# A fused QKV projection on one NeuronCore: block-product columns 504 wide in rows of 512, direct columns 288 wide in two banks

## The chip, the cores and the metric

The kernel runs on one core of one Trainium2 chip. The metric is the device time of one execution in microseconds (us). Three runs of the kernel before the change took 362.86, 363.02 and 363.09 us; their median, 363.02 us, is the time that the change is measured against.

## The reference

```python
"x": np.random.randn(16, 512, 768).astype(np.float32)
"w_qkv": np.random.randn(768, 3 * 768).astype(np.float32)

def reference(x, w_qkv):
    qkv = np.matmul(x, w_qkv)
    hidden = x.shape[-1]
    q = qkv[..., :hidden]
    k = qkv[..., hidden:2*hidden]
    v = qkv[..., 2*hidden:]
    return np.stack([q, k, v], axis=0).astype(np.float32)
```

So 8192 rows of 768 elements are multiplied by a weight of 768 by 2304, and the 2304 result columns are stored as three outputs of 768 columns each.

## The kernel before

**Rows.** The 8192 rows are worked off in 32 pairs of 128 rows (`NP` = 32, index `p`). The contraction of 768 is cut into six slices of 128 (`KT` = 6), or two halves of three (`KH` = 3).

**Columns.** The 2304 columns are cut into five ranges: two groups (`q` = 0 and 1) of two column blocks each, a block being `CB` = 512 columns, and between the groups a remainder of `REM` = 2304 - 4 * 512 = 256 columns, the *direct columns*. Group 0 starts at column 0, the direct columns at 1024, group 1 at 1280.

**First stage.** The first three row pairs (`NS` = 3) are multiplied plainly, in bf16, by `block` (line 375): for each of the four column blocks there are six row tiles of six matmuls (line 385). While it runs, the weights arrive and are turned into what the main stage needs: bf16 copies `b1`, a copy `b22` and four sums and differences `t` of weight blocks (`sum_w`, line 105), the last two kinds in float32r, a 4-byte type.

**Main stage.** The other 29 row pairs (p = 3 to 31) use a scheme with seven block products instead of eight: the pair's 256 rows and a group's 1024 columns are a two by two arrangement of blocks (a `Quad`), and `do(u, n)` (line 220) makes product `n` by `product` (line 201), three matmuls into one PSUM bank each (line 212). Products 1 and 2 take bf16 operands (`xb`, `b1`), products 3 to 7 float32r operands (sums of x blocks in `s`, and `t` or `b22`). A pass over one row pair handles both groups (`two`, line 275; `last`, line 309, for the final pair), so it has 2 x 7 x 3 = 42 block-product matmuls, of which 30 are float32r and 12 bf16. ScalarE copies results out of PSUM (lines 226, 233, 239, 243), VectorE adds others on top (lines 230, 240, 246), into an output tile `o` of 2 x 1024 columns, which `store_quad` (line 251) stores by two DMAs on SyncE's queue.

**Direct columns.** In every pass `rem(p)` (line 267) makes the 256 direct columns in bf16 without the scheme: `rem_row` (line 260) issues six matmuls for each of the two row tiles, 12 in all (line 262). Both row tiles lie in one PSUM bank of 512 float32 (`[P, 2, REM]`), and one ScalarE instruction copies them out (line 272).

**Order.** The order on each engine is that of the program text (a manual schedule). PSUM banks come from one pool of eight, `ps_pool`, in rotation: a pass takes seven (two for `x`, one for the direct columns, two for `z`, two for `y`). A bank is given out again when the last reader of its former content is done. In a pass the order on TensorE is: products 1 of both groups, the direct columns, products 2, 6, then 5, 7, 5, 7, then 4, 3 of group 0 and 4, 3 of group 1.

**Start.** Before the first data are there, TensorE multiplies a tile of zeros (`busy`, line 361: 11 matmuls, later 4 more), between the transposes of the first two row pairs (`turn_rows`, line 160).

**SBUF layout.** The tiles `b1`, `b22`, `t` and the pool `tq` start at multiples of 2048 bytes of a partition; the bf16 weights of the direct columns lie in two tiles, `w_rem0` before `b1` and `w_rem1` in a pool of its own ahead of the pool of `s`.

Of the kernel before, what the change touches and what calls it, by code (L numbers as in the profile page):

```python
# [10 lines left out]
def kernel(  # L11
# [20 lines left out]
    nc = tc.nc  # L32
    P = 128
# [5 lines left out]
    KT = K // P  # L39
    KH = KT // 2  # L40
    KC = K // 4
    NP = M // (2 * P)
    CB = 512
    REM = N3 - 4 * CB
    Q_OFF = (0, 2 * CB + REM)
    R_OFF = 2 * CB
    fp32 = mybir.dt.float32
    f32r = mybir.dt.float32r
    bf16 = mybir.dt.bfloat16
    ident = mybir.ActivationFunctionType.Identity  # L50
    add = mybir.AluOpType.add
# [13 lines left out]
    xin_pool = ctx.enter_context(tc.tile_pool(name="xin", bufs=3))  # L65
    xf_pool = ctx.enter_context(tc.tile_pool(name="xf", bufs=2))
    xb_pool = ctx.enter_context(tc.tile_pool(name="xb", bufs=4))
    rem_pool = ctx.enter_context(tc.tile_pool(name="rem", bufs=1))
    s_pool = ctx.enter_context(tc.tile_pool(name="s", bufs=2))
    ps_pool = ctx.enter_context(tc.tile_pool(name="ps", bufs=8, space=bass.MemoryType.PSUM))  # L70

# [1 line left out]

    tiny = w_pool.tile([P, 1], fp32, name="tiny")
    eye = w_pool.tile([P, 176], bf16, name="eye")[:, :P]
    w_rem = [w_pool.tile([P, KH, REM], bf16, name="w_rem0"), None]

    b1 = [w_pool.tile([P, KT, CB], bf16, name=f"b1_{q}") for q in range(2)]
    b22 = [w_pool.tile([P, KH, CB], f32r, name=f"b22_{q}") for q in range(2)]
    t_0 = w_pool.tile([P, 4, KH, CB], f32r, name="t_0")  # L80
    w_rem[1] = rem_pool.tile([P, KH, REM], bf16, name="w_rem1")
    ts = [[t_0[:, n] for n in range(4)], None]


# [2 lines left out]
    def load_w(dst, j0, nj, off, cols):  # L87
        rows = w_qkv.rearrange("(p j) n -> p j n", j=KT)
        nc.sync.dma_start(dst, rows[:, j0:j0 + nj, off:off + cols])

    stage = {}

    def load_blocks(q, c, nj=KH):
        if q == 0:
            t = tq_pool.tile([P, KT, CB], fp32, name="st0", tag="tq")
            for j in range(0, KT, nj):
                load_w(t[:, j:j + nj], j, nj, Q_OFF[q] + c * CB, CB)
            stage[q, 0, c], stage[q, 1, c] = t[:, :KH, :], t[:, KH:, :]
        else:
            for h in range(2):  # L100
                t = st_pool.tile([P, KH, CB], fp32, name="st1", tag="st")
                load_w(t[:], h * KH, KH, Q_OFF[q] + c * CB, CB)
                stage[q, h, c] = t[:]

    def sum_w(q, n):
        t1, t2, t3, t4 = ts[q]
# [8 lines left out]
    xin, xf, xb, sr = {}, {}, {}, {}  # L115
# [78 lines left out]
    def quad(p, q):  # L194
        u = Quad()
        u.p, u.q = p, q
        u.o = o_pool.tile([P, 2, 2 * CB], fp32, name="o", tag="o")
        u.x = u.y = u.z = None
        return u

    def product(u, n, ps, start):
        t1, t2, t3, t4 = ts[u.q]
        if n <= 2:
            h = (n - 1) * KH
            lhs = [xb[u.p][:, h + j, :P] for j in range(KH)]
            rhs = [b1[u.q][:, h + j, :] for j in range(KH)]
        else:
            k, t = {3: (4, b22[u.q][:]), 4: (0, t4), 5: (1, t1), 6: (2, t2), 7: (3, t3)}[n]
            lhs = [sr[u.p][:, k, j, :] for j in range(KH)]
            rhs = [t[:, j, :] for j in range(KH)]  # L210
        for j in range(KH):
            nc.tensor.matmul(  # L212
                ps[:], lhs[j], rhs[j],
                start=(start and j == 0), stop=(j == KH - 1), skip_group_check=True,
            )

    def bank():
        return ps_pool.tile([P, CB], fp32, name="ps")

    def do(u, n):  # L220
        c11, c12 = u.o[:, 0, :CB], u.o[:, 0, CB:]
        c21, c22 = u.o[:, 1, :CB], u.o[:, 1, CB:]
        if n == 1:
            u.x = bank()
            product(u, 1, u.x, True)
            nc.scalar.activation(c11, u.x[:], ident)  # L226
        elif n == 2:
            u.z = bank()
            product(u, 2, u.z, True)
            nc.vector.tensor_tensor(c11, c11, u.z[:], op=add)  # L230
        elif n == 6:
            product(u, 6, u.x, False)
            nc.scalar.activation(c12, u.x[:], ident)  # L233
        elif n == 5:
            u.y = bank()
            product(u, 5, u.y, True)
        elif n == 7:
            product(u, 7, u.x, False)
            nc.scalar.activation(c22, u.x[:], ident)  # L239
            nc.vector.tensor_tensor(c22, c22, u.y[:], op=add)  # L240
        elif n == 4:
            product(u, 4, u.x, False)
            nc.scalar.activation(c21, u.x[:], ident)  # L243
        elif n == 3:
            product(u, 3, u.y, False)
            nc.vector.tensor_tensor(c12, c12, u.y[:], op=add)  # L246
# [13 lines left out]
    def rem_row(p, r, ps):  # L260
        for j in range(KT):
            nc.tensor.matmul(  # L262
                ps, xb[p][:, j, r * P:(r + 1) * P], w_rem[j // KH][:, j % KH, :],
                start=(j == 0), stop=(j == KT - 1), skip_group_check=True,
            )

    def rem(p):
        ps = ps_pool.tile([P, 2, REM], fp32, name="ps")
        for r in range(2):
            rem_row(p, r, ps[:, r, :])  # L270
        o = or_pool.tile([P, 2, REM], fp32, name="orem")
        nc.scalar.activation(o[:], ps[:], ident)  # L272
        nc.sync.dma_start(rows_of(1, p, R_OFF - H, R_OFF - H + REM), o[:])

    def two(a, b, early):
# [33 lines left out]
    def last(a, b):  # L309

        p = a.p

        def rem_stored(r):
            ps = bank()
            rem_row(p, r, ps[:, :REM])
            o = or_pool.tile([P, 2, REM], fp32, name="orem")
            nc.scalar.activation(o[:, 0, :], ps[:, :REM], ident)  # L317
# [24 lines left out]


    NS = 3
    zero = xb_pool.tile([P, CB], bf16, name="zero", tag="xb")
    nc.vector.memset(zero[:], 0.0)  # L346
    load_rows(0)
    nc.scalar.activation(tiny[:], zero[:, :1], ident)
# [26 lines left out]
    def block(q, c, w, groups, cast_next):  # L375


        ps = {}
        for js, tiles in groups:
            for n in tiles:  # L380
                p, r = divmod(n, 2)
                if n not in ps:
                    ps[n] = bank()
                for j in js:
                    nc.tensor.matmul(  # L385
                        ps[n][:], xb[p][:, j, r * P:(r + 1) * P], w[:, j, :],
                        start=(j == 0), stop=(j == KT - 1), skip_group_check=True,
                    )
# [5 lines left out]
                nc.scalar.activation(u.o[:, r, c * CB:(c + 1) * CB], ps[n][:], ident)  # L394
                if c == 1 and r == 1:
                    store_quad(u)

# [28 lines left out]
    act.activation(w_rem[1][:], st_rem[:, KH:], ident)  # L426
    dve.tensor_copy(out=w_rem[0][:], in_=st_rem[:, :KH])
    bt0 = bt_pool.tile([P, KT, CB], bf16, name="bt")
    bt1 = bt_pool.tile([P, KT, CB], bf16, name="bt")

    block(0, 0, b1[0], singles, nothing)
    rem(0)
# [5 lines left out]
        cast(0, h, 1, bt0, dve)  # L438
    for n in range(1, 5):
        sum_w(0, n)  # L440
    dve.tensor_copy(out=b22[0][:], in_=stage[0, 1, 1])
# [5 lines left out]
    t_1 = [tq_pool.tile([P, 2, KH, CB], f32r, name=f"t_1{n}", tag="tq") for n in range(2)]  # L447
    ts[1] = [t_1[n // 2][:, n % 2] for n in range(4)]
    sum_w(1, 1)
    sum_w(1, 2)  # L450
# [2 lines left out]
    sums_x(3)  # L453
    sum_w(1, 3)
    sum_w(1, 4)
    dve.tensor_copy(out=b22[1][:], in_=stage[1, 1, 1])

    for p in range(NS, NP):
        def early():
# [41 lines left out]
```

## Time and profile before

| | |
|---|---|
| median of 3 runs | 363.02 us |
| span of the profiled execution, first to last instruction | 361.3 us |
| between the two | 1.7 us |
| TensorE busy | 353.4 us (98%) |
| VectorE, ScalarE, GpSimd busy | 224.4, 182.9, 173.9 us (62, 51, 48%) |
| float32r block-product matmuls, 128x512 (line 212) | 870 in the program |
| bf16 matmuls, 128x512 (lines 212 and 385) | 348 and 144 in the program |
| bf16 matmuls of the direct columns, 128x256 (line 262) | 384 in the program |
| granted TensorE clock | 1.000 over the span |

One profiled execution gives all rows but the first and the counts. Matmuls are pipelined: the duration of a matmul's record is longer than the time until the next one starts, so costs of matmuls are read below as the step from one start to the next. A few matmul records are missing from the trace (28 of 348 bf16 records of line 212), so a group of 42 may show 41. In the timeline and chain views the first column is the start in us from the span's start, the second the length in us, and xN the number of instructions merged into the line.

### The profile page before, as it was taken

The page shows a single profiled execution, that of the slowest core. Times are in us where ns is not written, and L with a number is a line of the kernel's source. Part 1 is how long each engine was busy: PE and PEld are TensorE (multiplying, and loading weights), DVE is VectorE, ACT ScalarE, POOL GpSimd, SP SyncE. Part 2 cuts the span into 40 slices and gives each one's busy share as a digit, 9 for nine tenths or more (in the row PEclk, how much of TensorE's full clock was granted, in tenths as well). Part 3 has the DMA queues.
Part 4 walks back from the last instruction along what each step waited for, and adds up shares of the span by engine and source line. Part 5 has one row for each costly group of instructions (what it writes and reads, how often), then busy time and mean ns, then how long its engine had stood idle before and what let it go on. Part 6 is the DMA issues. An engine that isn't in the chain of part 4 may idle for free.

```text
span 361.3 us, 5221 instructions
## 1 busy us (share of the span) xinstructions
PE 353.4 (98%) x1765; PEld 251.0 (69%) x1797; DVE 224.4 (62%) x239; ACT 182.9 (51%) x304; POOL 173.9 (48%) x180
## 2 busy tenths in 40 slices
PE   8999999999999999999999999999999999999995
PEld 3644577777777777777777777777777777777763
DVE  3499826765566765566675565676556676556642
ACT  4547555455454545454545445455545454545452
POOL 0001861746664445664445665444665444666410
PEclk9999999999999999999999999999999999999999
DMA  7999869988898999899899999998989899999666
GB/s 298 405 388 373 286 221 359 331 289 295 278 328 301 294 273 294 276 324 315 280 280 290 281 308 309 291 289 278 292 288 321 295 300 271 297 272 339 264 261 232
DMA packets 80617, 108.08 MB, mean 299 GB/s; under 512 B 4816, under 2 KB 60368, under 8 KB 80592
## 3 DMA queue, kind: packets, MB, share of 16 engines
q1 hardware_dynamic: 65184, 96.35, 80.8%
q10 hardware_dynamic: 15408, 11.41, 9.6%
q8 instruction: 14, 0.23, 0.3%
q14 instruction: 11, 0.09, 0.1%
HBM read 32.24 MB, written 75.50 MB: 298 GB/s over the span
## 4 chain that ended last, share of the span: by engine, by line
PE 96%; ACT 1%; issue 1%; ACTq 0%; DVE 0%
PE ps L212 75%; PE ps L262 11%; PE ps L385 9%; PE ps L365 1%; PE ps L167 1%; ACT o L243 0%; ACTq L303 0%; ACT xb L147 0%; ACT orem L317 0%; DVE xb L145 0%; ACT xc L147 0%; ACTq L319 0%; DVE zero L346 0%; ACTq L317 0%
## 5 line engine op out<-in xcount | busy, mean ns | idle before, releaser
L212 PE MATMUL ps<-t,s 128*128 128x512 f32 x696 | 173.8, 398 | 0.0
L212 PEld LDWEIGHTS ps<-t,s 128*128 128x128 f32 x696 | 130.7, 188 | 29.7
L175 POOL CAST xb<-xf 128x1536 bf16<-128x1536 f32 x29 | 43.8, 1510 | 168.3 <-DVE xf L130 156.0
L240 DVE TENSOR_TENSOR o<-o,ps 128x512 f32<-128x512 f32 x58 | 39.9, 688 | 91.2 <-ACT o L239 91.2
L130 DVE STREAM_TRANSPOSE xf<-xin 128x1536 f32<-128x1536 f32 x29 | 85.5, 2950 | 3.7 <-DMA out_dram<-orem 2.1
L212 PE MATMUL ps<-b,xb 128*128 128x512 bf16 x320 | 82.4, 380 | 1.5
L239 ACT ACTIVATE o<-ps 128x512 f32<-128x512 f32 x58 | 34.8, 600 | 44.2 <-PE ps L212 44.2
L212 PEld LDWEIGHTS <-xb 128*128 128x128 bf16 x348 | 31.7, 98 | 35.6 <-issue 7.3
L233 ACT ACTIVATE o<-ps 128x512 f32<-128x512 f32 x58 | 34.9, 601 | 42.1 <-PE ps L212 39.4
L246 DVE TENSOR_TENSOR o<-o,ps 128x512 f32<-128x512 f32 x58 | 39.9, 688 | 21.3 <-PE ps L212 20.2
L212 PE MATMUL ps<-b,s 128*128 128x512 f32 x174 | 48.7, 389 | 0.0
L262 PE MATMUL ps<-w_rem,xb 128*128 128x256 bf16 x384 | 47.2, 273 | 0.0
L243 ACT ACTIVATE o<-ps 128x512 f32<-128x512 f32 x58 | 34.7, 599 | 24.1 <-PE ps L212 21.3
L226 ACT ACTIVATE o<-ps 128x512 f32<-128x512 f32 x58 | 34.7, 598 | 23.8 <-DVE o L246 20.6
L262 PEld LDWEIGHTS <-xb 128*128 128x128 bf16 x384 | 37.4, 98 | 11.2 <-issue 0.5
L230 DVE TENSOR_TENSOR o<-o,ps 128x512 f32<-128x512 f32 x58 | 36.5, 673 | 5.4 <-PE ps L212 4.1
L212 PEld LDWEIGHTS ps<-b,s 128*128 128x128 f32 x174 | 32.7, 188 | 6.8
L184 POOL TENSOR_TENSOR s<-s,xf 128x384 fp32r<-128x384 f32 x29 | 30.0, 1035 | 2.3
L183 POOL TENSOR_TENSOR s<-xf 128x384 fp32r<-128x384 f32 x29 | 30.9, 1064 | 0.0
L185 POOL TENSOR_TENSOR s<-xf 128x384 fp32r<-128x384 f32 x29 | 29.5, 1017 | 0.0
L187 POOL TENSOR_TENSOR s<-xf,s 128x384 fp32r<-128x384 f32 x29 | 29.5, 1016 | 0.0
L272 ACT ACTIVATE orem<-ps 128x512 f32<-128x512 f32 x31 | 18.5, 598 | 20.7 <-PE ps L262 19.5
(36 smaller groups left out, 129.4 us busy)
## 6 DMA issues: line engine op xcount, KB each, us to landing
out_dram<-o SPq DMA_DIRECT2D x62, 768.0 KB, 4.8
out_dram<-o SPq DMA_DIRECT2D x65, 256.0 KB, 4.1
xin<-in_x_dram SPq DMA_DIRECT2D x62, 192.0 KB, 6.9
xin<-in_x_dram ACTq DMA_DIRECT2D x54, 192.0 KB, 4.4
out_dram<-orem SPq DMA_DIRECT2D x31, 256.0 KB, 5.7
st<-in_w_qkv_dram SPq DMA_DIRECT2D x6, 768.0 KB, 13.1
xin<-in_x_dram SPq DMA_DIRECT2D x3, 768.0 KB, 5.7
st<-in_w_qkv_dram SPq DMA_DIRECT2D x6, 256.0 KB, 6.1
```

The source lines that it names most:

```text
L130: nc.vector.transpose(t[:].rearrange("p j (g b) -> p g j b", b=G), xin.pop(p)[:].rearrange("p g (a j) -> p g j a", a=G),)
L175: nc.gpsimd.tensor_copy(out=xb[p][:], in_=xf[p][:])
L212: nc.tensor.matmul(ps[:], lhs[j], rhs[j], start=(start and j == 0), stop=(j == KH - 1), skip_group_check=True,)
L226: nc.scalar.activation(c11, u.x[:], ident)
L230: nc.vector.tensor_tensor(c11, c11, u.z[:], op=add)
L233: nc.scalar.activation(c12, u.x[:], ident)
L239: nc.scalar.activation(c22, u.x[:], ident)
L240: nc.vector.tensor_tensor(c22, c22, u.y[:], op=add)
L243: nc.scalar.activation(c21, u.x[:], ident)
L246: nc.vector.tensor_tensor(c12, c12, u.y[:], op=add)
L262: nc.tensor.matmul(ps, xb[p][:, j, r * P:(r + 1) * P], w_rem[j // KH][:, j % KH, :], start=(j == 0), stop=(j == KT - 1), skip_group_check= ...
L385: nc.tensor.matmul(ps[n][:], xb[p][:, j, r * P:(r + 1) * P], w[:, j, :], start=(j == 0), stop=(j == KT - 1), skip_group_check=True,)
```

## The change

`CB`, the width of a column block, becomes 504, and a new `CP` = 512 is the pitch: every tile that holds column blocks keeps rows of 512 elements, of which 504 are used. `REM` becomes 2304 - 4 * 504 = 288. Two row tiles of 288 columns need 576 float32 and no longer fit one bank, so `rem` takes one bank for each row tile and ScalarE copies each out by itself; a pass now takes eight banks. The two `w_rem` tiles become one, which is filled up so that the tiles behind it still start at multiples of 2048 bytes; the pool `rem` goes. The second batch of start-up matmuls (4 bf16 of 512 columns) becomes 4 float32r matmuls of 496, 496, 480 and 480 columns on a new tile of zeros, which GpSimd fills first of all. The outputs' stores have the same number of DMAs; pieces that were 256 columns wide are 240, 264 or 288.

```diff
-    CB = 512
+    CB = 504
+    CP = 512
     REM = N3 - 4 * CB
...
-    rem_pool = ctx.enter_context(tc.tile_pool(name="rem", bufs=1))
...
-    w_rem = [w_pool.tile([P, KH, REM], bf16, name="w_rem0"), None]
-
-    b1 = [w_pool.tile([P, KT, CB], bf16, name=f"b1_{q}") for q in range(2)]
-    b22 = [w_pool.tile([P, KH, CB], f32r, name=f"b22_{q}") for q in range(2)]
-    t_0 = w_pool.tile([P, 4, KH, CB], f32r, name="t_0")
-    w_rem[1] = rem_pool.tile([P, KH, REM], bf16, name="w_rem1")
+    w_rem = w_pool.tile([P, 7 * P * 2], bf16, name="w_rem")[:, :KT * REM]
+    w_rem = w_rem.rearrange("p (h j c) -> p h j c", h=2, j=KH)
+    w_rem = [w_rem[:, h] for h in range(2)]
+
+    b1 = [w_pool.tile([P, KT, CP], bf16, name=f"b1_{q}")[:, :, :CB] for q in range(2)]
+    b22 = [w_pool.tile([P, KH, CP], f32r, name=f"b22_{q}")[:, :, :CB] for q in range(2)]
+    t_0 = w_pool.tile([P, 4, KH, CP], f32r, name="t_0")[:, :, :, :CB]
...
-        u.o = o_pool.tile([P, 2, 2 * CB], fp32, name="o", tag="o")
+        u.o = o_pool.tile([P, 2, 2 * CP], fp32, name="o", tag="o")[:, :, :2 * CB]
...
-    def bank():
-        return ps_pool.tile([P, CB], fp32, name="ps")
+    def bank(n=CB):
+        return ps_pool.tile([P, CP], fp32, name="ps")[:, :n]
...
     def rem(p):
-        ps = ps_pool.tile([P, 2, REM], fp32, name="ps")
+        o = or_pool.tile([P, 2, REM], fp32, name="orem")
         for r in range(2):
-            rem_row(p, r, ps[:, r, :])
-        o = or_pool.tile([P, 2, REM], fp32, name="orem")
-        nc.scalar.activation(o[:], ps[:], ident)
+            ps = bank(REM)
+            rem_row(p, r, ps)
+            nc.scalar.activation(o[:, r, :], ps, ident)
         nc.sync.dma_start(rows_of(1, p, R_OFF - H, R_OFF - H + REM), o[:])
...
-    zero = xb_pool.tile([P, CB], bf16, name="zero", tag="xb")
+    zeros = bt_pool.tile([P, 2 * CP], f32r, name="zeros", tag="bt")
+    nc.gpsimd.memset(zeros[:].bitcast(mybir.dt.uint32), 0)
+    zero = xb_pool.tile([P, CP], bf16, name="zero", tag="xb")
...
-            nc.tensor.matmul(ps[:], zero[:, :P], zero[:], start=True, stop=True)
+            nc.tensor.matmul(ps, zero[:, :P], zero[:, :CB], start=True, stop=True)
+
+    def busy_rounded():
+
+        ps = bank()
+        for n in (496, 496, 480, 480):
+            nc.tensor.matmul(
+                ps[:, :n], zeros[:, CP:CP + P], zeros[:, :n], start=True, stop=True
+            )
...
-    busy(4)
+    busy_rounded()
```

More of the change, by code (lines that the diff above doesn't have):

```diff
@@ L94, in load_blocks @@
         if q == 0:
-            t = tq_pool.tile([P, KT, CB], fp32, name="st0", tag="tq")
+            t = tq_pool.tile([P, KT, CP], fp32, name="st0", tag="tq")[:, :, :CB]
             for j in range(0, KT, nj):
@@ L100, in load_blocks @@
             for h in range(2):
-                t = st_pool.tile([P, KH, CB], fp32, name="st1", tag="st")
-                load_w(t[:], h * KH, KH, Q_OFF[q] + c * CB, CB)
-                stage[q, h, c] = t[:]
+                t = st_pool.tile([P, KH, CP], fp32, name="st1", tag="st")[:, :, :CB]
+                load_w(t, h * KH, KH, Q_OFF[q] + c * CB, CB)
+                stage[q, h, c] = t
     def sum_w(q, n):
@@ L207, in product @@
         else:
-            k, t = {3: (4, b22[u.q][:]), 4: (0, t4), 5: (1, t1), 6: (2, t2), 7: (3, t3)}[n]
+            k, t = {3: (4, b22[u.q]), 4: (0, t4), 5: (1, t1), 6: (2, t2), 7: (3, t3)}[n]
             lhs = [sr[u.p][:, k, j, :] for j in range(KH)]
@@ L212, in product @@
             nc.tensor.matmul(
-                ps[:], lhs[j], rhs[j],
+                ps, lhs[j], rhs[j],
                 start=(start and j == 0), stop=(j == KH - 1), skip_group_check=True,
             )
-    def bank():
-        return ps_pool.tile([P, CB], fp32, name="ps")
+    def bank(n=CB):
+        return ps_pool.tile([P, CP], fp32, name="ps")[:, :n]
     def do(u, n):
@@ L225, in do @@
             product(u, 1, u.x, True)
-            nc.scalar.activation(c11, u.x[:], ident)
+            nc.scalar.activation(c11, u.x, ident)
         elif n == 2:
@@ L229, in do @@
             product(u, 2, u.z, True)
-            nc.vector.tensor_tensor(c11, c11, u.z[:], op=add)
+            nc.vector.tensor_tensor(c11, c11, u.z, op=add)
         elif n == 6:
             product(u, 6, u.x, False)
-            nc.scalar.activation(c12, u.x[:], ident)
+            nc.scalar.activation(c12, u.x, ident)
         elif n == 5:
@@ L238, in do @@
             product(u, 7, u.x, False)
-            nc.scalar.activation(c22, u.x[:], ident)
-            nc.vector.tensor_tensor(c22, c22, u.y[:], op=add)
+            nc.scalar.activation(c22, u.x, ident)
+            nc.vector.tensor_tensor(c22, c22, u.y, op=add)
         elif n == 4:
             product(u, 4, u.x, False)
-            nc.scalar.activation(c21, u.x[:], ident)
+            nc.scalar.activation(c21, u.x, ident)
         elif n == 3:
             product(u, 3, u.y, False)
-            nc.vector.tensor_tensor(c12, c12, u.y[:], op=add)
+            nc.vector.tensor_tensor(c12, c12, u.y, op=add)
     def rows_of(s, p, lo, hi):
@@ L313, in rem_stored @@
         def rem_stored(r):
-            ps = bank()
-            rem_row(p, r, ps[:, :REM])
+            ps = bank(REM)
+            rem_row(p, r, ps)
             o = or_pool.tile([P, 2, REM], fp32, name="orem")
-            nc.scalar.activation(o[:, 0, :], ps[:, :REM], ident)
+            nc.scalar.activation(o[:, 0, :], ps, ident)
             row = (2 * p + r) * P
@@ L385, in block @@
                     nc.tensor.matmul(
-                        ps[n][:], xb[p][:, j, r * P:(r + 1) * P], w[:, j, :],
+                        ps[n], xb[p][:, j, r * P:(r + 1) * P], w[:, j, :],
                         start=(j == 0), stop=(j == KT - 1), skip_group_check=True,
@@ L393, in block @@
                 u = quads[q][p]
-                nc.scalar.activation(u.o[:, r, c * CB:(c + 1) * CB], ps[n][:], ident)
+                nc.scalar.activation(u.o[:, r, c * CB:(c + 1) * CB], ps[n], ident)
                 if c == 1 and r == 1:
@@ L425 @@
         cast_k(j)
[L426 to L429, printed above, removed]
+    act.activation(w_rem[1], st_rem[:, KH:], ident)
+    dve.tensor_copy(out=w_rem[0], in_=st_rem[:, :KH])
+    bt0 = bt_pool.tile([P, KT, CP], bf16, name="bt")[:, :, :CB]
+    bt1 = bt_pool.tile([P, KT, CP], bf16, name="bt")[:, :, :CB]
     block(0, 0, b1[0], singles, nothing)
@@ L440 @@
         sum_w(0, n)
-    dve.tensor_copy(out=b22[0][:], in_=stage[0, 1, 1])
+    dve.tensor_copy(out=b22[0], in_=stage[0, 1, 1])
     block(0, 1, bt0, halves(range(6)), cast_next(1, 0, b1[1]))
@@ L446 @@
     rem(2)
-    t_1 = [tq_pool.tile([P, 2, KH, CB], f32r, name=f"t_1{n}", tag="tq") for n in range(2)]
+    t_1 = [
+        tq_pool.tile([P, 2, KH, CP], f32r, name=f"t_1{n}", tag="tq")[:, :, :, :CB] for n in range(2)
+    ]
     ts[1] = [t_1[n // 2][:, n % 2] for n in range(4)]
@@ L455 @@
     sum_w(1, 4)
-    dve.tensor_copy(out=b22[1][:], in_=stage[1, 1, 1])
+    dve.tensor_copy(out=b22[1], in_=stage[1, 1, 1])
     for p in range(NS, NP):
```

## The prediction

> **What bounds the kernel now.** I read the page's busy shares first, then the chain of work that ended last, then that chain in order of time, and last the timeline of TensorE and its weight loads inside one pass.
>
> ```profile
> PE 353.4 (98%) x1765; PEld 251.0 (69%) x1797; DVE 224.4 (62%) x239; ACT 182.9 (51%) x304; POOL 173.9 (48%) x180
> PE 96%; ACT 1%; issue 1%; ACTq 0%; DVE 0%
> PEclk9999999999999999999999999999999999999999
> ```
>
> TensorE is busy for 98% of the span, and 96% of the chain is its own work, at the full granted clock throughout. No other engine is above 62%. What the change is worth is therefore the sum of TensorE's own steps, unless something else comes to hold TensorE up.
>
> ```profile
> 9.46 2.16 PE ps L385 x10
> 57.47 1.31 PE ps L262 x12
> 58.83 9.38 PE ps L212 x41
> 68.21 1.31 PE ps L262 x12
> 69.57 9.38 PE ps L212 x41
> ```
>
> This is the chain in order of time. Ten bf16 matmuls of 512 columns take 2.16 us: 216 ns from one start to the next. Twelve bf16 matmuls of 256 columns take 1.31 us: 109.2 ns each. A pass is 68.21 - 57.47 = 10.74 us, and 69.57 + 9.38 = 78.95 is the next pass's start, so passes follow each other without a hole. In a pass 12 x 109.2 ns are direct columns (1.31 us) and 12 x 216 ns are products 1 and 2 (2.59 us); the other 30, in float32r, share 10.74 - 1.31 - 2.59 = 6.84 us, or 228.0 ns each. Between the same width in bf16 and in float32r there are thus 12 ns, and the two timelines below show that these are not a constant.
>
> ```profile
> 64.70 0.84 PE L212 MATMUL ps<-b,s 128*128 128x512 f32 x3
> 65.38 0.84 PE L212 MATMUL ps<-t,s 128*128 128x512 f32 x3
> 66.06 0.84 PE L212 MATMUL ps<-b,s 128*128 128x512 f32 x3
> 66.74 1.47 PE L212 MATMUL ps<-b,xb 128*128 128x512 bf16 x6
> 68.05 1.47 PE L262 MATMUL ps<-w_rem,xb 128*128 128x256 bf16 x12
> ```
>
> ```profile
> 59.91 1.57 PEld L212 LDWEIGHTS ps<-t,s 128*128 128x128 f32 x7
> 61.75 2.68 PEld L212 LDWEIGHTS ps<-t,s 128*128 128x128 f32 x12
> ```
>
> Late in a pass three float32r matmuls take 0.68 us (64.70, 65.38, 66.06): 226.7 ns each. The weight loads, which start with the matmul before them and last 0.19 us, tell the same: the twelve from 61.75 on are (2.68 - 0.19) / 11 = 226 ns apart, but the first seven of the pass (1.57 - 0.19) / 6 = 230 ns. Equal instructions of equal shape first wander around 230 ns and then settle at 226.7 ns. The records' durations (shortest, median, longest) show the same, from 60.1 us on and from 62.2 us on:
>
> ```profile
> L212 PE MATMUL ps<-t,s x7: 387/393/397, 60.1 to 61.5; 128*128 128x512 f32 x7
> L212 PE MATMUL ps<-t,s x14: 389/389/389, 62.2 to 65.8; 128*128 128x512 f32 x14
> ```
>
> **The change part by part: what the widths do.** One column in bf16 costs (216 - 109.2) / 256 = 0.417 ns, so 8 columns are 3.3 ns and 32 columns 13.3 ns. Counts are the program's, over all passes and the first stage.
>
> Direct columns: 384 matmuls go from 256 to 288 columns, 109.2 to 122.5 ns: 384 x 13.33 ns = +5.12 us. All of them stand on the chain, none is hidden.
>
> bf16 blocks: 348 in products 1 and 2 and 144 in the first stage lose 8 columns: 492 x 3.33 ns = -1.64 us.
>
> float32r products: 870 matmuls lose 8 columns. This decides, since the two terms above leave +3.48 us, and 3.48 us / 870 = 4.0 ns is what each of them has to save for the kernel to stay even. No row shows a float32r matmul of any width but 512, so I bound it. From above: the step doesn't follow the width and stays where it was (226.7 settled, 228.0 on average), saving nothing; it can even lose, if it never settles and stays at the 230 ns of the pass's first seven (+2.0 ns). From below: the whole excess over bf16 goes and the step is 216 - 3.3 = 212.6 ns, a saving of 15.4 ns. In between, the plain reading from the nearest row, in proportion or with a fixed excess, saves 3.3 to 3.5 ns. I do not take the plain reading, because the excess is neither: it varies between instructions of one shape and then locks. The settled 226.7 ns is 34 times 6.67 ns, the time of 16 columns at 0.417 ns; all widths of the kernel so far are multiples of 16 columns, and 8 columns are half of that. If the step settles on such multiples, the next places are 33 (220.0 ns) and 34 (226.7 ns). I take 220.0, also nearly the middle of 212.6 and 226.7: -6.67 ns x 870 = -5.80 us. This is a choice between ends far apart, and the range keeps both.
>
> The sum is 5.12 - 1.64 - 5.80 = -2.32 us.
>
> The Trainium skill, "TensorE: Matmul & The Clock Gate", section "Wait — 56ns, not 53.3ns?", gives the start-to-start step of a warm matmul as N / 2.4 GHz plus about 2.5 ns for back-to-back matmuls. The bf16 rows obey it, and the float32r row at 226.7 ns does not, where the rule has 215.8. The rule speaks against this change: by it every matmul pays for its columns alone, and 42 x -3.33 + 12 x 13.33 = +20 ns a pass, or an estimated +0.6 us in all.
>
> **What else is added, and what hides it.** ScalarE's copies of the direct columns, one of 512 columns before (line 272), two of 288 after:
>
> ```profile
> L272 ACT ACTIVATE orem<-ps 128x512 f32<-128x512 f32 x31 | 18.5, 598 | 20.7 <-PE ps L262 19.5 <-PE ps L212 1.3
> L317 ACT ACTIVATE orem<-ps 128x256 f32<-128x256 f32 x2 | 0.8, 385 | 1.5 <-PE ps L262 1.5
> 66.26 0.60 ACT L243 ACTIVATE o<-ps 128x512 f32<-128x512 f32 x1 [0.76 <-PE ps L212]
> ```
>
> Before, one copy of 598 ns. After, two, each 385 + 32 x (598 - 385) / 256 = 412 ns, +0.23 us a pass. ScalarE is idle for half of each pass (51% busy), so nothing waits; without that cover it would be 29 x 0.23 = 6.6 us.
>
> The bank: a pass takes eight of eight banks instead of seven, so each bank returns to the same use one pass later. The tightest is product 1 of group 1, which needs the bank that ScalarE's copy of product 4 (line 243) frees at 66.26 + 0.60 = 66.86 us. That product's matmuls start three bf16 steps after 66.74, at 67.39: 0.53 us of slack. The others have more. Were it gone, each pass would wait by what is missing.
>
> DMA: issues stay the same in number on every queue (242 on SyncE's, 59 on ScalarE's) and so do the bytes; only pieces of 256 columns become 240, 264 or 288. The direct weights grow by an eighth and are loaded ahead of the third row pair, the first column block shrinks by 1.6%. The direct weights' cast (line 426) ran from 12.91 to 13.75 and is needed at 14.48; at 0.1 MB more over the 405 GB/s of the page's second slice it starts some 0.2 us later and lasts 0.1 us longer: done by about 14.1.
>
> The weights' casts and sums read three rows of 504 where they read one run of 1536. The VectorE cast of that size took 953 ns (line 373) and 1745 ns at the slowest (line 456, to float32r). The first cast starts at 18.70 us, and TensorE has its twelve 512-column steps from 18.05 on, to 20.64, before it needs it: 1745 ns would still be in time.
>
> Start: GpSimd clears 1024 words ahead of the identity; the 128-column clear took 0.21 us, so eight times that, 1.7 us, bounds it. The identity was ready at 1.30 us and is first used at 5.49 us. The four float32r dummies replace four bf16 ones that ended before TensorE waited 0.53 us for ScalarE's cast; up to that much is free.
>
> All these I cost at nothing.
>
> **How this stands to the median.** The profiled execution spans 361.3 us, and 1.7 us lie around it up to the median of 363.02 us. My sum leaves a span of 359.0 us and a time of 360.7 us.
>
> **Rivals.** A, the excess goes: the step becomes 212.6 ns, -15.4 x 870 = -13.4 us, with the other terms -9.9 us: 353.1 us. For it: bf16 shows that the array can take a column every 0.417 ns, and the wandering records (387 to 397 ns for one shape) show that the excess is not a constant. Against it: no float32r matmul in the trace comes near 216. B, slower, the lock holds: the step stays at 34 x 6.67 ns although 8 columns are gone, and the kernel keeps only the bill of +3.48 us: 366.5 us. For it: once settled, all records of a pass have one duration to the nanosecond. It decides as soon as a float32r matmul saves less than 4.0 ns, that is, as soon as the average step stays above 224.0 ns. C, the plain reading: 3.3 to 3.5 ns saved, +0.4 to +0.6 us, 363.5 us, no change. D, it never settles: a width off the multiples of 16 keeps every step at 230 ns, 870 x 2.0 = +1.7 on top of 3.48: 368.2 us.
>
> **How the numbers follow.** Chances: my forecast 0.31, A 0.21, B 0.22, C 0.14, D 0.09, anything else (a bank or a load that comes late) 0.03. A measurement of this kernel can tell about 0.2%, 0.73 us, from no change. Faster are the forecast and A, 0.52; C is within 0.2% in two cases of three and otherwise just slower: same 0.09; slower 0.39. The predicted time is the forecast's, 360.7 us. The range takes in A and B with their ends, 352.9 to 367.0; it leaves out D and the rest. The forecast alone would lie in 359.5 to 362 us.
>
> **What would show it.** Right: the float32r steps of a settled stretch at 220 ns, three in 0.66 us, twelve direct matmuls in 1.47 us, six bf16 steps in 1.28 us, a pass of 10.66 us. Three float32r steps in 0.64 us mean A, in 0.68 us B, in 0.67 us C, in 0.69 us D. A hole before product 1 of group 1 would show the bank's slack mis-costed. The prediction is wrong if the pass is longer than 10.74 us or shorter than 10.5 us.

## The result and the profile after

| | before | after |
|---|---|---|
| median of 4 runs each | 362.94 us (362.71 to 363.09) | 365.63 us (365.44 to 365.86) |
| ratio, 95% interval | | 1.008 [1.0066, 1.0094] |
| span of the profiled execution | 361.3 us | 364.1 us |
| one pass of the main loop | 10.740 us | 10.840 us |
| first direct product of the main loop starts at | 46.56 us | 46.43 us |

The kernel became slower by 0.8%, 2.7 us. (A fourth run of the kernel before, 362.71 us, moves its median from 363.02 to 362.94 us.) One execution of all those told of below, the profiled one of the variant with narrower bf16 blocks, ran at a mean granted clock of 0.753 and took 455.54 us; it is left out of that variant's time. The span grew by 2.8 us: 29 passes of 0.100 us more are 2.9 us, and the first stage ends 0.13 us earlier. The page of after, the rows that answer to those shown of before, with the three groups whose widths changed:

```profile
PE 358.0 (98%) x1797; PEld 251.4 (69%) x1797; DVE 225.8 (62%) x239; ACT 185.5 (51%) x335; POOL 174.3 (48%) x181
...
PEclk9999999999999999999999999999999999999999
...
PE 98%; ACT 0%; DVE 0%; issue 0%
...
L213 PE MATMUL ps<-t,s 128*128 128x504 f32 x696 | 172.9, 396 | 0.0
...
L263 PE MATMUL ps<-w_rem,xb 128*128 128x288 bf16 x384 | 52.3, 286 | 0.0
...
L273 ACT ACTIVATE orem<-ps 128x288 f32<-128x288 f32 x62 | 23.1, 410 | 15.8 <-PE ps L263 14.8
```

TensorE still is the whole chain, at the full granted clock, and its matmuls of both kinds have no idle time before them (the last column, 0.0). So no wait was added: the time is in TensorE's own steps. The chain of after in order of time (start, length, what):

```profile
57.45 1.47 PE ps L263 x12
58.92 9.37 PE ps L213 x42
68.29 1.47 PE ps L263 x12
69.76 9.37 PE ps L213 x42
```

Twelve direct matmuls take 1.47 us where they took 1.31, and the 42 of the block products 9.37 where they took 9.43 (10.74 - 1.31). A pass is 68.29 - 57.45 = 10.84 us: the 160 ns that the direct columns cost are there, and of the blocks' 42 narrower matmuls only 60 ns came back. (The chain view puts the start of a piece 0.16 us later than the timeline does, 68.29 against 68.13 below; the steps are the same in both.) The timeline of TensorE in the same pass of after says which of them gave nothing:

```profile
64.79 0.84 PE L213 MATMUL ps<-b,s 128*128 128x504 f32 x3
65.47 0.84 PE L213 MATMUL ps<-t,s 128*128 128x504 f32 x3
66.15 0.84 PE L213 MATMUL ps<-b,s 128*128 128x504 f32 x3
66.84 1.45 PE L213 MATMUL ps<-b,xb 128*128 128x504 bf16 x6
68.13 1.63 PE L263 MATMUL ps<-w_rem,xb 128*128 128x288 bf16 x12
```

Three float32r matmuls start 0.68 us apart (64.79, 65.47, 66.15), as before: 226.7 ns each, although each has eight columns fewer. The six bf16 matmuls take 68.13 - 66.84 = 1.29 us, 1.31 before. What did go in float32r is the wandering at the start of a pass. The weight loads of after, and the durations (shortest, median, longest) of the float32r records of TensorE that start in 60.3 to 65.9 us:

```profile
59.82 4.71 PEld L213 LDWEIGHTS ps<-t,s 128*128 128x128 f32 x21
```

```profile
L213 PE MATMUL ps<-t,s x23: 388/388/388, 60.3 to 65.9; 128*128 128x504 f32 x23
```

The 21 loads are (4.71 - 0.19) / 20 = 226 ns apart from the first on, where the first seven of before were 230 ns apart, and all records have one length, where the first seven of before had 387 to 397 ns.

The starts of the single instructions in one pass, read from the two traces, close the sum (sums over the same 54 matmuls):

| steps of one pass | before | after | difference |
|---|---|---|---|
| 12 direct matmuls | 1310 ns | 1470 ns | +160 |
| 12 bf16 matmuls of products 1 and 2 | 2413 | 2379 | -34 |
| 30 float32r matmuls: first step | 418 | 410 | -8 |
| the next six | 224, 231, 236, 228, 232, 231 | six of 226.7 | -22 |
| the following 22 | 226.7 each | 226.7 each | 0 |
| the last step | 230 | 234 | +4 |
| sum | 10740 | 10840 | +100 |

(The last bf16 matmul ahead of a float32r one has a step of only 28 ns, and the first float32r step is longer by as much; neither is a price by itself.)

### The profile page after: what moved, and what is told of

Same layout as the page of the kernel before. It is cut to its first block, busy times and chain, and to the rows that moved or that the text cites. A ratio compares the mean times of both kernels' runs of the same rounds, so it can differ in the third digit from the quotient of the medians.

```text
span 364.1 us, 5288 instructions
## 1 busy us (share of the span) xinstructions
PE 358.0 (98%) x1797; PEld 251.4 (69%) x1797; DVE 225.8 (62%) x239; ACT 185.5 (51%) x335; POOL 174.3 (48%) x181
## 4 chain that ended last, share of the span: by engine, by line
PE 98%; ACT 0%; DVE 0%; issue 0%
PE ps L213 75%; PE ps L263 13%; PE ps L396 8%; PE ps L368 1%; PE ps L168 1%; ACT xb L148 0%; DVE xb L146 0%; ACT xc L148 0%; ACT orem L318 0%; DVE zero L349 0%
## 5 line engine op out<-in xcount | busy, mean ns | idle before, releaser
L213 PE MATMUL ps<-t,s 128*128 128x504 f32 x696 | 172.9, 396 | 0.0
L241 DVE TENSOR_TENSOR o<-o,ps 128x504 f32<-128x504 f32 x58 | 39.4, 679 | 94.4 <-ACT o L240 94.4
L213 PE MATMUL ps<-b,xb 128*128 128x504 bf16 x348 | 83.8, 377 | 0.0
L234 ACT ACTIVATE o<-ps 128x504 f32<-128x504 f32 x58 | 34.3, 592 | 46.1 <-PE ps L213 43.6
L240 ACT ACTIVATE o<-ps 128x504 f32<-128x504 f32 x58 | 34.4, 594 | 44.5 <-PE ps L213 44.5
L247 DVE TENSOR_TENSOR o<-o,ps 128x504 f32<-128x504 f32 x58 | 39.4, 679 | 22.2 <-PE ps L213 20.7
L263 PE MATMUL ps<-w_rem,xb 128*128 128x288 bf16 x384 | 52.3, 286 | 0.0
L213 PE MATMUL ps<-b,s 128*128 128x504 f32 x174 | 48.8, 389 | 0.0
L244 ACT ACTIVATE o<-ps 128x504 f32<-128x504 f32 x58 | 34.3, 592 | 24.4 <-PE ps L213 21.5
L227 ACT ACTIVATE o<-ps 128x504 f32<-128x504 f32 x58 | 34.3, 591 | 24.0 <-DVE o L247 20.8
L231 DVE TENSOR_TENSOR o<-o,ps 128x504 f32<-128x504 f32 x58 | 37.9, 675 | 5.1 <-PE ps L213 3.7
L273 ACT ACTIVATE orem<-ps 128x288 f32<-128x288 f32 x62 | 23.1, 410 | 15.8 <-PE ps L263 14.8
```

The lines of the kernel that those rows point to most:

```text
L213: nc.tensor.matmul(ps, lhs[j], rhs[j], start=(start and j == 0), stop=(j == KH - 1), skip_group_check=True,)
L227: nc.scalar.activation(c11, u.x, ident)
L231: nc.vector.tensor_tensor(c11, c11, u.z, op=add)
L234: nc.scalar.activation(c12, u.x, ident)
L240: nc.scalar.activation(c22, u.x, ident)
L241: nc.vector.tensor_tensor(c22, c22, u.y, op=add)
```

## The experiments

Two kinds of kernel were run. Three benches time stretches of 24 matmuls of one kind with 6 or so bf16 matmuls between, and nothing else of the kernel; nine variants of the kernel undo or do one part. Each bench ran once, at the full granted clock. For a bench the step is the mean of the last 14 steps of a stretch, taken from the starts of single instructions. Variants were timed in several rounds, beside runs of the kernel before on the same chip.

### Does the float32r step follow the width?

The bench's core, with three rows of float32r in turn, each with its own weights:

```python
    def run(n, cols, off=0, woff=0, same=False, rows=3):
...
            rhs = mov[:].rearrange("p a b -> p (a b)")[:, k * 512 + off:k * 512 + off + cols]
            lhs = wts[:].rearrange("p a b -> p (a b)")[:, k * P + woff:k * P + woff + P]
            nc.tensor.matmul(ps[i // 3 % 2][:, :cols], lhs, rhs, start=True, stop=True)
...
    last = run(24, 504)
    plain(6)
```

> Leaves out the projection: it only runs stretches of 24 float32r matmuls of one width each (512, 508, 504, 500, 496, 492, 488, 484, 480, 472, 464, 448, 416, 384, 320, 256 columns), with 6 bf16 matmuls of 512 columns between the stretches. Read the settled step, start to start, of each stretch. Lock on a grid: the step does not follow the width but stays on one value for a range of widths and then falls by a whole grid step. On a grid of 13.33 ns (32 columns): 226.7 ns for 512 down to 484, 213.3 ns for 480 to 452, 200.0 ns at 448. On a grid of 6.67 ns (16 columns): 226.7 for 512 to 500, 220.0 for 496 to 484, 213.3 for 480. Rival, a floor (something of 226.7 ns that has nothing to do with the columns, such as the weight load and its handover): 226.7 ns at all widths down to some 480 and below. Rival, a cost per column: 223 ns at 504, 219.5 at 496, 212.5 at 480, without plateaus.

The timeline of TensorE in this bench, six of its sixteen stretches (start, length of 24 matmuls):

```profile
18.22 5.82 PE L72 MATMUL ps<-mov,wts 128*128 128x512 f32 x24
...
31.77 5.80 PE L72 MATMUL ps<-mov,wts 128*128 128x504 f32 x24
...
38.52 5.79 PE L72 MATMUL ps<-mov,wts 128*128 128x500 f32 x24
...
45.28 5.71 PE L72 MATMUL ps<-mov,wts 128*128 128x496 f32 x24
...
71.85 5.55 PE L72 MATMUL ps<-mov,wts 128*128 128x480 f32 x24
...
113.44 3.21 PE L72 MATMUL ps<-mov,wts 128*128 128x256 f32 x24
```

From 512 to 504 columns 24 matmuls get shorter by 0.02 us, where eight columns at 0.417 ns would be 24 x 3.33 ns = 0.08 us; from 504 to 496 they get shorter by 0.09. The steps:

| columns | 512 | 508 | 504 | 500 | 496 | 492 | 488 | 484 | 480 | 472 | 464 | 448 | 416 | 384 | 320 | 256 |
|---|---|---|---|---|---|---|---|---|---|---|---|---|---|---|---|---|
| step, ns | 226.6 | 227.6 | 226.6 | 226.7 | 223.6 | 222.1 | 225.7 | 218.4 | 216.7 | 213.4 | 210.0 | 202.4 | 188.6 | 173.4 | 146.6 | 120.0 |
| above bf16 | 10.8 | 13.4 | 14.1 | 15.9 | 14.4 | 14.6 | 19.9 | 14.2 | 14.2 | 14.2 | 14.2 | 13.2 | 12.8 | 10.9 | 10.8 | 10.8 |

The second row takes off 0.4167 ns a column and 2.5 ns, which is what the two bf16 widths of before follow (216 and 109.2 ns). The widths fall into two kinds. At 512, 504, 472, 384, 320 and 256 the steps settle on one value, and that value is a multiple of 6.67 ns: 34, 34, 32, 26, 22 and 18 of them; for 512, 384, 320 and 256 that is one for each 16 columns and two more. At the other ten widths the steps go round a cycle to the end of the stretch (at 500 between 225 and 228, about the same mean of 226.7; at 496 between 220 and 227; at 464 between 205 and 215). So the multiples are real where a step settles, but 504 and 472, which lie halfway between two multiples of 16, both settle on the upper one, and the next width on the multiples, 496, does not settle on the lower one, 220.0, but averages 223.6. A floor, a step that has nothing to do with the columns, it is not either: 480 columns take 216.7 ns and 256 take 120.0. Beside 512 columns, every width from 508 down to 416 saves less than bf16 would; the excess over bf16 is smallest, 10.8 ns, at 512, 384, 320 and 256.

### Do the conditions inside the kernel make the step?

The same bench at 512 columns, with the moving rows or the weights shifted, with one row or six in place of three, and with other bf16 matmuls ahead of each stretch.

```diff
+    last = run(24, 512, off=8)
...
+    last = run(24, 512, woff=8)
...
+    last = run(24, 512, same=True)
...
+    plain(12, 288)
+    last = run(24, 512)
```

> Leaves out the projection: stretches of 24 float32r matmuls of 512 columns under one changed condition each (moving rows shifted by 32, 64, 128 and 512 bytes; weights shifted by 32, 64 and 128 bytes; one row and one weight tile throughout; six rows in place of three), then stretches behind 1 to 8 bf16 matmuls, behind bf16 matmuls of 504, 288, 256 and 496 columns, and single float32r matmuls between single bf16 ones. Grid lock: every stretch settles at 226.7 ns, and only the number of steps until it settles differs with what ran before it. If the addresses made the excess: some of the shifted stretches settle elsewhere, towards 216 ns or above 227 ns.

What stands ahead of a stretch (1 to 8 bf16 matmuls, of 512, 504, 496, 288 or 256 columns) leaves the settled step at 226.6 to 227.0 ns and changes only how many steps wander before it, about two to nine. One row throughout or six rows: 227.0. A single float32r matmul between single bf16 ones makes 460 ns a pair, 17 ns more than 216 and 226.7. But the place of the operands counts: moving rows shifted by 32, 64 or 128 bytes took 233.4, 228.6 and 232.4 ns, by 512 bytes again 226.6; weights shifted by 32, 64 or 128 bytes 233.4, 233.3 and 232.4.

That asked for a finer look at the shifts, since a better place than the kernel's might exist:

> Leaves out the projection: stretches of 24 float32r matmuls of 512 columns (some of 504 and 496), moving rows and weights shifted alone or together by 16 to 1024 bytes from the 512-byte places they have in the kernels. If the relative place of the two makes the excess: equal shifts of both settle at 226.7 ns as unshifted ones do, and shifts of one alone are slower, as 32, 64 and 128 bytes were (229 to 234 ns). If each one's own place counts: equal shifts are slow too. If some place is better than the kernels' own, a stretch settles below 226.7 ns, down to 216 ns.

The timeline of TensorE in that bench: unshifted; moving rows by 16 bytes; by 256 bytes; weights by 192 bytes; both by 64 bytes:

```profile
17.26 5.80 PE L72 MATMUL ps<-mov,wts 128*128 128x512 f32 x24
...
24.02 5.91 PE L72 MATMUL ps<-mov,wts 128*128 128x512 f32 x24
...
51.59 5.82 PE L72 MATMUL ps<-mov,wts 128*128 128x512 f32 x24
...
85.88 5.86 PE L72 MATMUL ps<-mov,wts 128*128 128x512 f32 x24
...
113.17 5.81 PE L72 MATMUL ps<-mov,wts 128*128 128x512 f32 x24
```

One instruction, one width, and in these five stretches 24 of them take 5.80 to 5.91 us by where the operands lie. Both benches together, at 512 columns, by the place of the moving row less that of the weights, modulo 256 bytes:

| bytes | 0 | 16 | 32 | 48 | 64 | 96 | 128 | 160 | 192 | 224 | 240 |
|---|---|---|---|---|---|---|---|---|---|---|---|
| step, ns | 226.6 to 227.0 | 231.8 | 233.4 | 233.4 | 228.6, 228.9 | 233.4 | 232.4 to 233.4 | 234.3 | 233.3, 233.3 | 233.4 | 233.4 |

Moving rows by +64 and weights by +192 (less by 192 is 64 more, modulo 256) agree, 228.6 and 228.9, and shifting both alike by 32, 64, 128 or 256 bytes changes nothing (226.6 to 226.9). So in these stretches the step goes by the distance between the two, modulo 256 bytes, and none of the places tried is better than 0, whose 226.7 ns is also the settled step of the kernel before and after: none of them would gain anything for its tiles. At 504 columns shifts of 16 and 32 bytes left the mean at 226.7; at 496 columns shifts of 32 and 64 bytes raised it from 223.6 to 224.5 and 226.7.

### One part of the change at a time

The float32r products alone at 504 columns, the rest as before (the first of each product's three stays at 512 in one product, so 28 of 30 in a pass are narrower):

```diff
+        w = (512,) * KH if n <= 2 else (512 if n == 5 else 504, 504, 504)
...
-                ps[:], lhs[j], rhs[j],
+                ps[:, :w[j]], lhs[j], rhs[j][:, :w[j]],
```

> The kernel before, with 28 of the 30 float32r matmuls of a pass on 504 of their 512 columns (the last 8 columns of the blocks then lack most of products 3 to 7). A cost per column, or a fixed excess over bf16: 28 x 3.33 = 93 ns a pass, -2.7 us, 360.0 us. A step that does not fall from 512 to 504: passes of 10.74 us or up to 25 ns less where the wandering at their start goes, 0 to -0.7 us.

Measured 363.31 us against 362.59, 1.0011 [1.0002, 1.002]. The chain in order of time:

```profile
57.55 1.31 PE ps L263 x12
58.86 9.44 PE ps L213 x42
68.30 1.31 PE ps L263 x12
```

A pass is 10.75 us (10.747 from the starts of single instructions), 7 ns longer than before: 0.2 us in 29 passes, and the rest of the measured difference is no more than the spread of the kernel before (362.51 to 363.30 us). Its steps are 413, then 226.7 for five, then a wander of eleven (230, 233, 225, 229, 230, ...), then 226.7 again. The wander begins at the 512-wide matmul of product 5 and its first five steps come again at the second one, so the mix of two widths, which the change doesn't have, may make it; its eleven steps are 27 ns longer than settled ones. The settled 504-wide steps are 226.7 ns, as at 512. Eight columns less in 812 float32r matmuls took nothing off a settled step. This is the run that decides on the prediction's largest term.

The direct columns alone at 288, blocks left at 512, each row tile in a bank of its own (32 columns are computed twice and not stored):

```diff
-    REM = N3 - 4 * CB
-    Q_OFF = (0, 2 * CB + REM)
+    CP = 512
+    REM = 288
+    Q_OFF = (0, 2 * CB + 256)
...
```

> The kernel before in its column blocks of 512, with the direct columns 288 wide in two banks as in the change; the 32 columns more are computed in excess and not stored. A cost per column in bf16: 12 x 13.33 = 160 ns a pass and 36 x 13.33 ns in the first stage, +5.1 us, 367.8 us. If the wider direct columns were partly hidden: less than +4 us.

Measured 367.61 against 362.59 us, 1.013 [1.0113, 1.0147], +5.0 us. The chain in order of time:

```profile
58.02 1.47 PE ps L263 x12
59.49 9.43 PE ps L213 x42
68.92 1.47 PE ps L263 x12
```

10.90 us a pass, +160 ns, all of it in the twelve direct matmuls; the block products are as before, 9.43 us. Nothing hides them.

The bf16 block products alone at 504, eight of twelve in a pass:

```diff
+        w = (512, 504, 504) if n <= 2 else (512, 512, 512)
...
-                ps[:], lhs[j], rhs[j],
+                ps[:, :w[j]], lhs[j], rhs[j][:, :w[j]],
```

> The kernel before, with 8 of the 12 bf16 product matmuls of a pass on 504 of their 512 columns (the second and third of each product; the last 8 columns of the group's blocks then lack two thirds of products 1 and 2). Cost per column in bf16: 8 x 3.33 = 27 ns a pass, 29 passes: -0.8 us. If the bf16 widths also set how the float32r stretch of a pass starts: the steps at its start change too, and the pass moves by up to another 25 ns either way, -1.5 to 0 us.

Measured 362.32 (the median of the nine executions at full clock) against 362.59 us, 0.9992 [0.9983, 1.0002]: -0.27 us, with an interval from -0.6 to +0.1. That is less than the -0.8 us expected and can't be told from nothing, so the term isn't settled by this run. Its one trace is that of the execution at a clock of 0.753, so its steps can't be set against the others. A saving of 27 ns a pass can be lost in the wandering: in the benches of the places and of the conditions, the first ten steps of two unshifted stretches of 512 columns, each behind six bf16 matmuls of 512, sum to 2481 and 2505 ns. That this happened here is not shown. The term's size is shown by the step table of after (-34 ns a pass) and by the last pair of runs below, both of which include it.

The two banks and the two copies alone, on the kernel before:

```diff
-        ps = ps_pool.tile([P, 2, REM], fp32, name="ps")
-        for r in range(2):
-            rem_row(p, r, ps[:, r, :])
...
-        nc.scalar.activation(o[:], ps[:], ident)
+        for r in range(2):
+            ps = bank()
+            rem_row(p, r, ps[:, :REM])
+            nc.scalar.activation(o[:, r, :], ps[:, :REM], ident)
```

> The kernel before, 512 and 256 columns, with only the two banks and the two ScalarE copies for the direct columns. If these are hidden, as the prediction had it: 363.0 us within 0.4 and passes of 10.74 us. If the eighth bank of eight makes TensorE wait: a hole before product 1 of group 1 in each pass, and up to the +2.7 us that the change cost.

Measured 362.95 against 362.62 us, 1.0006 [0.9996, 1.0015]; passes of 10.740 us to the nanosecond. Hidden, as costed.

The change with the old start-up matmuls:

```diff
-    busy_rounded()
+    busy(4)
```

> The changed kernel with the four bf16 dummies of before in place of the four float32r ones. If the start-up matmuls do not matter: the same time as the changed kernel, 365.6 us within 0.4, and passes of 10.84 us. If they set the phase in which each pass enters its float32r stretch: the settled step stays 226.7 ns, but passes differ by the wandering steps, 10.84 to 10.87 us, up to +0.9 us.

Measured 365.76 against 362.62 us, 1.0081 [1.0064, 1.0097]; passes of 10.840 us. The start-up matmuls neither cost nor bring anything that the later passes show.

### Can the change be saved?

By another width, 496, with 320 direct columns:

```diff
-    CB = 504
+    CB = 496
...
```

(The direct weights, now 320 columns, are in two tiles again, two slices in one and four in the other, and `o` has rows of 2 x 496.)

> The changed kernel with column blocks of 496 and direct columns of 320. Bf16 terms against the kernel before: 12 x -6.67 and 12 x 26.67 ns, +240 ns a pass. If the float32r step is what the stretch at 496 columns showed by itself, 223.5 ns on average: 30 x -4.5 = -135 ns, so +105 ns a pass, +3.0 us, 365.7 us. If it locks on the next multiple of 6.67 ns, 220.0 ns: -240 ns and no change, 362.7 us. If it stays at 226.7 ns: -39 and +240, +5.8 us.

Measured 366.27 against 362.59 us, 1.0096 [1.0081, 1.0111]. Passes of 10.854 and 10.859 us, +117 ns on average: 12 x 26.7 = +320 ns of direct columns, against about 203 that came back. The float32r steps go round between 218 and 227 ns, much as at 496 in the bench. Twice the columns moved costs a little more than 504 did.

By rows of 504 in place of 512 for the float32r tiles, so that columns and rows end together:

```diff
-    b22 = [w_pool.tile([P, KH, CP], f32r, name=f"b22_{q}")[:, :, :CB] for q in range(2)]
-    t_0 = w_pool.tile([P, 4, KH, CP], f32r, name="t_0")[:, :, :, :CB]
+    b22 = [w_pool.tile([P, KH, CB], f32r, name=f"b22_{q}") for q in range(2)]
+    t_0 = w_pool.tile([P, 4, KH, CB], f32r, name="t_0")
...
```

> The changed kernel with the float32r tiles of weights in rows of 504 elements (2016 bytes) instead of 512, so that their places against the weight tiles of x differ by other multiples of 32 bytes. As the shifted stretches of 504 columns alone (226.7 ns on average at 16 and 32 bytes): no change, 365.6 us within 0.5, though the steps need not settle on one value. As the shifted stretches of 512 columns (229 to 234 ns): 870 x 2.5 to 7 ns, +2 to +6 us.

Measured 366.93 against 362.98 us, 1.0109 [1.0094, 1.0124], passes of 10.873 us, 33 ns longer than after. Rows of 2016 bytes lie at another distance from their weights from one row to the next, and the steps, between 224 and 233 ns, never settle. This fits the table of places in its direction; in size it is less than the shifts made of 512 columns (30 x 6 ns would be 180), as the two shifts at 504 columns in the bench were, too.

By taking float32r out. First the kernel before, with the sums and differences in bf16:

```diff
-    b22 = [w_pool.tile([P, KH, CB], f32r, name=f"b22_{q}") for q in range(2)]
-    t_0 = w_pool.tile([P, 4, KH, CB], f32r, name="t_0")
+    b22 = [w_pool.tile([P, KH, CB], bf16, name=f"b22_{q}") for q in range(2)]
+    t_0 = w_pool.tile([P, 4, KH, CB], bf16, name="t_0")
...
-        s = s_pool.tile([P, 5, KH, P], f32r, name="s")
+        s = s_pool.tile([P, 5, KH, P], bf16, name="s")
...
```

> The kernel before with its float32r tiles (the sums of x and w, and the copy of w) in bf16, so that all 42 product matmuls of a pass are bf16 of 512 columns; the results are rounded more coarsely. If the difference between the two types is the float32r step itself, 228.0 against 215.9 ns, 30 a pass: 12.1 x 870 = -10.5 us, 352.3 us, passes of 10.375 us. If other work (the 90% busy DMA, GpSimd's sums) stands right behind TensorE: holes between the matmuls and less than half of that.

Measured 352.54 us (352.18 to 352.66) against 362.98, 0.9709 [0.9693, 0.9725]. Then the change with the same edit:

> The changed kernel with bf16 in place of float32r in its sums of x and w and its copy of w, as was done to the kernel before; the results are rounded more coarsely. If bf16 follows the width at 0.417 ns a column and the float32r step was the whole difference between plan and result: passes of 42 x 212.5 + 12 x 122.5 ns = 10.395 us against 10.375 us for 512 columns in bf16, so 0.6 us more than that kernel, 353.1 us. If the two banks or the narrower pieces cost something that the float32r steps hid: passes above 10.41 us or holes between the matmuls.

Measured 352.54 us (352.53 to 352.58) against 362.57, 0.9722 [0.9705, 0.9738]. The chain in order of time, of the kernel before in bf16 and then of the change in bf16:

```profile
68.77 9.06 PE ps L212 x42
77.83 1.31 PE ps L262 x12
79.14 3.02 PE ps L212 x14
```

```profile
57.98 8.93 PE ps L213 x42
66.90 1.47 PE ps L263 x12
68.37 8.93 PE ps L213 x42
```

Now the blocks do give their columns back: 9.06 to 8.93 us, against 1.31 to 1.47. From the starts of single instructions a pass goes from 10.375 to 10.395 us, +20 ns, which is 42 x -3.33 + 12 x 13.33; the 0.6 us that 29 passes make of it are no larger than the two intervals, and in the profiled executions a first direct product of the main loop that starts 0.59 us earlier (46.54 and 45.95 us) takes them back (spans 350.9 and 350.8). In bf16 the change costs 20 ns a pass, and no difference that the measured times can tell. Both kernels beat before by some 10 us, at a coarser rounding of products 3 to 7; how much rounding is allowed decides whether they may be used.

## Why the prediction was wrong

The forecast was 360.7 us and faster; the kernel took 365.63 and was slower. The time lies within the range only because the range reached to rival B. By the prediction's own sign, a pass longer than 10.74 us, it was wrong: the pass is 10.84 us.

**The step that failed** is the choice of the float32r step: "I take 220.0, also nearly the middle of 212.6 and 226.7: -6.67 ns x 870 = -5.80 us". Measured, the settled step is 226.7 ns at 504 as at 512, in the change, with the float32r products alone, and in the bench. In the place of -5.80 us the float32r matmuls gave -0.75 us (29 x 26 ns), and all of that is wandering that went, none of it the settled step. The idea behind the choice was half right: where a step settles on one value, it lies on a multiple of 6.67 ns (six widths of six). But 504 columns lie halfway between two multiples of 16, and the step settled on the upper one. The prediction named both places and had no row that spoke for the lower. The middle of two bounds was used as if it were evidence. That the lower place isn't to be had even at 496 (223.6) was beyond what any row of before could show.

**Rival B came true in its mechanism**: the step stays, and only the bill is left. Its price of +3.48 us was larger than the +2.7 measured. The wandering at the start of a pass went with the new width, 26 ns a pass with the two end steps, 29 x 26 = 0.75 us, which B hadn't counted: 3.48 - 0.75 = 2.73. Two smaller differences nearly cancel: the bf16 blocks gave 6 ns a pass less than B had (0.17 us, below), and the main loop started 0.13 us earlier. The point from which it decides, an average float32r step above 224.0 ns, is passed: the 30 steps of before share 6.84 us and those of after 26 ns less, 227 ns each. Rival A (212.6), the plain reading C (0.67 us for three) and D (230, never settled) all fall by the rows of after: 0.68 us for three steps, settled from the second on.

**The direct columns**, +5.12 us: right. 160 ns a pass in after; alone they cost +5.0 us.

**The bf16 blocks**, -1.64 us: nearly right in size, on the evidence of the steps (29 x 34 ns in the passes and 144 x 3.33 ns ahead of them, some -1.5 us); the run of this part alone didn't show it. In the pass -34 ns in place of the -40 that twelve times 3.33 make, since two of the twelve steps, next to the float32r stretch, are set by it and not by their width (28 and 227 ns before, 29 and 226 after).

**What was costed at nothing** cost nothing. The copies: 410 ns each (412 were worked out), and the variant with them alone stayed even. The eighth bank: in after the copy of product 4 that frees it ends at 66.35 + 0.59 = 66.94 us and product 1 of group 1 starts 226 + 2 x 212.5 ns after 66.84, at 67.49, 0.55 us of slack (0.53 worked out). The direct weights' cast ends at 14.07 us (14.1), and the first direct matmul starts at 14.28, earlier than before, without having been held up. GpSimd's clear took 0.95 us (1.7 was the bound). These rows of ScalarE's and GpSimd's timelines of after show the three:

```profile
66.35 0.59 ACT L244 ACTIVATE o<-ps 128x504 f32<-128x504 f32 x1 [0.77 <-PE ps L213]
```

```profile
13.15 0.92 ACT L437 ACTIVATE w_rem<-str 128x864 bf16<-128x864 f32 x1 [2.89 <-DMA str<-in_w_qkv_dram]
```

```profile
0.73 0.95 POOL L347 MEMSET zeros<- 128x1024 uint32 x1 [0.29 <-POOLq L498]
```

**The page that spoke against the change** was the better guide to the sign. The Trainium skill, "TensorE: Matmul & The Clock Gate", section "Wait — 56ns, not 53.3ns?", has N / 2.4 GHz plus about 2.5 ns a matmul, and the estimate of +20 ns a pass that the prediction worked out from it is what the two bf16 kernels show (10.375 to 10.395 us). For float32r the runs differ from it, by 10.8 to some 20 ns a matmul, and the measurement decides: +100 ns.

What stays open: what makes the excess of a float32r matmul. The runs show that it depends on the distance between moving row and weights modulo 256 bytes, which speaks for two reads that get in each other's way. That is argued and not shown: no run separated a float32r matmul from its weight load.

## What to carry to other kernels

When an edit takes columns from one kind of matmul and gives them to another, price each kind by a step measured at the new width and in its own type: a sweep of widths in one bench of 120 us would have given the sign here, and a step at one width said nothing of its neighbour. Where a cost must be chosen between two bounds with no row that favours either, work out the break-even first (4.0 of 15.4 ns here) and let the chances, not the middle, carry the doubt. Before float32r is tuned by its widths, see whether the product needs it: taking it away was worth 10 us, the two widths tried nothing.

## What the runs showed that was not expected

- The step of a float32r matmul of 512 columns is 226.7 ns or 229 to 234 ns by the distance between its moving row and its weights, modulo 256 bytes. A distance of a multiple of 256 bytes is the best found.
- Eight or twelve columns fewer than 512 cost the same 226.7 ns on average in float32r, and 488 columns (225.7 ns) cost more than 492 (222.1) and 496 (223.6).
- Equal float32r matmuls need two to nine steps to settle after bf16 ones, by what stands ahead of them; at 504 columns in the change they settled at once.
